# RWKV recurrence of a hybrid block: two pairs of matmul pieces issued as one piece each, with a new table of scheduling offsets

## The chip, the cores and the metric

The kernel runs on one core of a Trainium2 chip. The core has a matmul engine (PE, with its weight loads shown as PEld), a vector engine (DVE), a scalar engine (ACT), a general engine (POOL) and a queue that issues transfers (SP). Each works through its own list of instructions in the order in which the program gives them, and waits on semaphores for the others. The metric is the device time of one execution in microseconds (us); lower is better.

## The reference, cut to what matters

The program computes two layers of a block with three branches (windowed attention, an RWKV-7 recurrence, retention), a gated mix of them, and a feed-forward part, for 256 tokens and a model width of 1024, in float32. The change touches the recurrence, which has 8 heads of 64 columns:

```python
def step(S, inp):
    r_t, w_t, k_t, v_t, a_t, b_t = inp
    Sa = jnp.einsum('bhvk,bhk->bhv', S, a_t)
    S = S * w_t[:, :, None, :] + Sa[..., None] * b_t[:, :, None, :] + v_t[..., None] * k_t[:, :, None, :]
    return S, jnp.einsum('bhvk,bhk->bhv', S, r_t)
_, y = lax.scan(step, S0, xs)
mu = jnp.mean(y, axis=-1, keepdims=True)
var = jnp.mean(jnp.square(y - mu), axis=-1, keepdims=True)
y = ((y - mu) * lax.rsqrt(var + RWKV_LN_EPS)).reshape(B, T, RWKV_WIDTH)
y = y * lnx_g + lnx_b
y = (y + bonus) * g
```

The result of this branch is multiplied by `w_rwkv_o` and goes into the mix.

## The kernel before, in words

**Big matmuls.** Nearly all the work is matrix products with large weights. Each weight block of 512 KB is loaded into `raw`, ACT rounds it to the fast float format (`wh`), DVE takes the rest (`wl = raw - wh`), and PE multiplies three times (`wh` with the high part of the activations, `wl` with the high part, `wh` with the low part) to keep float32 accuracy. These are the matmuls whose weights or moving operand are `wh` or `wl`; there are 3984 of them, and they are called the big matmuls here. Their outputs are named by the product: `gt` the gates, `po` the three output projections, `px` the output of the mix, `pfg`, `pfu`, `pd` the feed-forward part, `pf`, `aq`, `rq`, `rk`, `rv`, `rg` the input projections. (`pd` is also the name of a small tile of the recurrence.)

**Small pieces.** Everything else on PE (transposes, attention scores, the recurrence) is put between big matmuls.

**The order.** The program is first recorded, operation by operation (`Program.add`), and then put in order by a list scheduler that knows the engines, the buffers and rough costs (`forward`). For each engine it takes the ready operation with the highest key. For most small operations the key is the length of the work that still hangs on it plus an offset by the name of the output, from the table `PRI` (line 31). The order is fixed when the program is built: on the chip an engine takes its instructions in this order, whatever happens. `rec.together()` records the matmuls in its block as one operation, which the scheduler can't cut.

**The recurrence** is done in four chunks of 64 tokens (lines 1097 to 1148), each a chain: `pr` (the state with the keys, 8 matmuls of 64 columns) is copied to `RS` by ACT; `pu` multiplies `RS` by `M`, the inverse of the chunk's triangular matrix; ACT and DVE copy `pu` into `sv`, which then holds u beside the state; `pd` multiplies `sv` for the next state, and DVE scales that into the next chunk's `sv` (`SV`). The outputs are `py` (the state with r, 8 matmuls, copied into `ysb` by ACT) and `py2` (`sv` with `GR`, 8 matmuls, added to `ysb` by DVE). In the trace `py2` appears as `py` with `GR` as an operand.

**Behind the recurrence**, for each half t of the tokens, DVE takes the mean from `ysb` (`gmu`), ACT squares (`gsq`), DVE sums (`gvr`), POOL takes the power -1/2 (`ggr`), DVE multiplies by `ab` (made from `pgt`, the gate, and `lnx`), by `ggr`, and adds the other half of `ab`. PE transposes the result (`pto`, 4 transposes), ACT rounds it (`obh`) and DVE takes the rest (`obl`). Then come the big matmuls `po` with `obh` and `obl`. Half 0 of a weight block is multiplied by 6 big matmuls, then half 1 by 6.

All instructions that the scheduler emits carry line 454, the line of `emit`; so the views are read by tile names.

## Time and profile before

| what | before |
|---|---|
| median of 3 runs (lowest to highest) | 955.47 us (954.79 to 955.87) |
| the profiled execution: its own time, its span | 956.34 us, 954.5 us |
| mean granted PE clock | 1.000 |
| PE busy | 946.6 us, 99% of the span |
| DVE, ACT, POOL busy | 673.1, 532.5, 39.7 us |

Rows of the timeline give start, duration, engine, line, operation, output and inputs, shapes and a count of merged instructions; a bracket gives the idle time of that engine ahead of the row and what ended it. PE starts a matmul while the one before is still in the array, so the pace is read from starts, not from durations. A float32 matmul shows as two records: the 8 matmuls of `pr` are `x16`. A plain transpose is one record.

### The profile page before, as it was taken

The numbers are of one execution on the slowest core, as the hardware profiler recorded it, in microseconds if no ns is written. First come the engines' busy times: TensorE is split into PE (matmuls) and PEld (weight loads), VectorE is DVE, ScalarE is ACT, GpSimd is POOL, SyncE is SP. The second block draws the span as 40 slices with busy tenths as digits, with TensorE's granted clock in tenths as the row PEclk, the third lists the DMA queues.
The fourth block names the chain that finished last, engine by engine and source line by source line (L and its number), as shares of the span: only waits on it lengthen the run. The fifth ranks groups of instructions, "written<-read, shape, count | busy, mean of one in ns | idle before, by whom it ended". The sixth has DMA issues, their size and how long they took to land.

```text
span 954.5 us, 15127 instructions
## 1 busy us (share of the span) xinstructions
PE 946.6 (99%) x5906; PEld 791.4 (83%) x5906; DVE 673.1 (71%) x1030; ACT 532.5 (56%) x851; POOL 39.7 (4%) x37
## 2 busy tenths in 40 slices
PE   8999999999999999999999999999999999999998
PEld 6998787877888888898889988888778878888886
DVE  5889889878777555555468799988698665555443
ACT  6875876364547444444468757644645564444332
POOL 1110000000100000000010100000010000000000
PEclk9999999999999999999999999999999999999999
DMA  8656444543655666655553663545535556666562
GB/s 253 188 146 188 118 145 135 154 155 100 192 183 158 198 190 184 186 180 187 184 179 122 177 177 89 177 133 155 155 97 192 176 177 189 186 183 191 178 208 101
DMA packets 93425, 159.04 MB, mean 167 GB/s; under 512 B 5830, under 2 KB 26666, under 8 KB 93354
## 3 DMA queue, kind: packets, MB, share of 16 engines
q1 hardware_dynamic: 93354, 158.08, 54.7%
q8 instruction: 46, 0.75, 0.3%
q14 instruction: 25, 0.20, 0.1%
HBM read 157.01 MB, written 1.05 MB: 166 GB/s over the span
## 4 chain that ended last, share of the span: by engine, by line
PE 94%; DMA 2%; ACT 1%; DVE 1%; issue 1%; SPq 0%; ACTq 0%
PE gt L454 14%; PE pd L454 13%; PE pfu L454 11%; PE pfg L454 11%; PE po L454 8%; PE pf L454 8%; PE px L454 5%; PE rg L454 2%; PE rv L454 2%; PE rk L454 2%; PE rq L454 2%; PE akv L454 1%; DMA raw<-in_w_in_dram 1%; PE aq L454 1%; PE pas L454 1%; PE ptf L454 1%
## 5 line engine op out<-in xcount | busy, mean ns | idle before, releaser
L454 DVE TENSOR_TENSOR wl<-raw,wh 128x1024 fp32r<-128x1024 f32 (+1 forms) x293 | 356.8, 1219 | 208.7 <-ACT wh L454 207.7
L454 ACT CAST wh<-raw 128x1024 fp32r<-128x1024 f32 (+1 forms) x293 | 306.3, 1047 | 311.6 <-PE pd L454 66.3
L454 PE MATMUL gt<-wh,hth 128*128 128x512 f32 x192 | 77.2, 402 | 0.0
L454 PE MATMUL gt<-wh,htl 128*128 128x512 f32 x192 | 76.5, 398 | 0.0
L454 PE MATMUL gt<-wl,hth 128*128 128x512 f32 x192 | 76.3, 398 | 0.0
L454 PE MATMUL pfg<-wl,hth 128*128 128x512 f32 (+1 forms) x192 | 72.6, 378 | 0.0
L454 PE MATMUL pfg<-wh,hth 128*128 128x512 f32 (+1 forms) x192 | 72.2, 376 | 0.0
L454 PE MATMUL pfg<-wh,htl 128*128 128x512 f32 (+1 forms) x192 | 71.7, 373 | 0.0
L454 PE MATMUL pfu<-wl,hth 128*128 128x512 f32 (+1 forms) x192 | 71.4, 372 | 0.0
L454 PE MATMUL pfu<-wh,htl 128*128 128x512 f32 (+1 forms) x192 | 71.3, 371 | 0.0
L454 PE MATMUL pfu<-wh,hth 128*128 128x512 f32 (+1 forms) x192 | 71.3, 371 | 0.0
L454 PE MATMUL pd<-wh,atl 128*128 128x512 f32 x176 | 69.3, 394 | 0.0
L454 PE MATMUL pd<-wh,ath 128*128 128x512 f32 x176 | 69.3, 394 | 0.0
L454 PE MATMUL pd<-wl,ath 128*128 128x512 f32 x176 | 69.1, 393 | 0.0
L454 PE MATMUL pf<-htl,wh 128*128 128x256 f32 x224 | 64.0, 286 | 0.0
L454 PE MATMUL pf<-hth,wl 128*128 128x256 f32 x224 | 63.9, 285 | 0.0
L454 PE MATMUL pf<-hth,wh 128*128 128x256 f32 x224 | 63.8, 285 | 0.0
L454 PEld LDWEIGHTS pf<-htl,wh 128*128 128x128 f32 x224 | 42.8, 191 | 0.4 <-issue 0.3
L454 PEld LDWEIGHTS pf<-hth,wl 128*128 128x128 f32 x224 | 42.8, 191 | 0.4 <-issue 0.3
L454 PEld LDWEIGHTS pf<-hth,wh 128*128 128x128 f32 x224 | 42.8, 191 | 0.1
L454 PEld LDWEIGHTS gt<-wl,hth 128*128 128x128 f32 x192 | 36.1, 188 | 7.6 <-issue 0.6
L454 PEld LDWEIGHTS gt<-wh,hth 128*128 128x128 f32 x192 | 36.1, 188 | 7.6 <-issue 0.2
(326 smaller groups left out, 1927.4 us busy)
## 6 DMA issues: line engine op xcount, KB each, us to landing
raw<-in_w_in_dram SPq DMA_DIRECT2D x119, 512.0 KB, 3.9
raw<-in_w_ffn_gate_dram SPq DMA_DIRECT2D x44, 512.0 KB, 4.1
raw<-in_w_ffn_up_dram SPq DMA_DIRECT2D x44, 512.0 KB, 3.7
raw<-in_w_ffn_down_dram SPq DMA_DIRECT2D x44, 512.0 KB, 3.6
raw<-in_w_out_dram SPq DMA_DIRECT2D x16, 512.0 KB, 3.6
raw<-in_w_attn_o_dram SPq DMA_DIRECT2D x8, 512.0 KB, 3.6
raw<-in_w_ret_o_dram SPq DMA_DIRECT2D x8, 512.0 KB, 3.7
raw<-in_w_rwkv_o_dram SPq DMA_DIRECT2D x8, 512.0 KB, 3.6
```

The lines of the kernel that those rows point to most:

```text
L454: fn(*args, **kw)
```

## The change

Three things change.

1. In each chunk, `py` is recorded in the same piece as `pr`, and `py2` in the same piece as `pd` (in the last chunk, where there is no `pd`, `py2` is alone). The number of matmuls stays.
2. The copies of `pu` into `sv` are recorded ahead of the copies of `py` into `ysb`.
3. `PRI` holds other offsets for other names, so the order changes in the whole program, not only in the recurrence.

```diff
 PRI = {
-    "PC": -83000, "Tn": -20000, "Y": 60000, "Zs": 16000, "amx": -8000, "cum": 49000, "gsq": 23000, "k2":
...
+    "M": -2000, "Sb": -20000, "Tt": 65000, "ab": -16000, "adn": -3000, "ass": -51000, "bv": -3000,
...
                 with rec.together():
-                    for p in range(4):
-                        for par in range(2):
-                            mm(pr[HR[par], p, :], X[p][:, par, c, 0:64], sv[:, p, par, :])
+                    for p, par in heads:
+                        mm(pr[HR[par], p, :], X[p][:, par, c, 0:64], sv[:, p, par, :])
+                    for p, par in heads:
+                        mm(py[HR[par], p, :], X[p][:, par, c, 64:128], sv[:, p, par, :])
                 RS = ST([128, 4, 64], "RS")
                 S.copy(RS, pr)
-                py = PS([128, 4, 64], "py")
-                with rec.together():
...
                 pu = PS([128, 4, 64], "pu")
...
+                S.copy(sv[HR[0], :, 0, :], pu[HR[0]])
+                V.tensor_copy(sv[HR[1], :, 1, :], pu[HR[1]])
                 yv = ysb[t].rearrange("p (a b) v -> p a b v", b=2)
                 for par in range(2):
                     S.copy(yv[rr, :, par, :], py[HR[par]])
-                S.copy(sv[HR[0], :, 0, :], pu[HR[0]])
-                V.tensor_copy(sv[HR[1], :, 1, :], pu[HR[1]])
...
+                with rec.together():
+                    for p, par in heads if c < 3 else ():
+                        mm(pd[HR[par], p, :], BKT[p // 2][:, p % 2, c, 64 * par:64 * par + 64], sv[:, p, par, :])
+                    for p, par in heads:
+                        mm(py2[HR[par], p, :], GR[HR[par], p, c, :], sv[HR[par], p, par, :])
...
-                py2 = PS([128, 4, 64], "py2")
-                with rec.together():
...
```

What the scheduler makes of it is seen where instructions stand. First PE in one chunk of the recurrence of layer 2, before; `gt` and `po` are big matmuls, the other rows the pieces of the chunk, and the last row is `py2`:

```order
L454 MATMUL pr<-SV,X 64x64 x8
L454 MATMUL py<-SV,X 64x64 x8
L454 MATMUL gt<-wl,hth 128x512
L454 MATMUL gt<-wh,htl 128x512
L454 MATMUL pu<-RS,M 64x64 x8
L454 MATMUL gt<-wh,hth 128x512
L454 MATMUL gt<-wl,hth 128x512
L454 MATMUL gt<-wh,htl 128x512
L454 MATMUL gt<-wh,hth 128x512
L454 MATMUL gt<-wl,hth 128x512
L454 MATMUL pd<-SV,BKT 64x64 x8
L454 MATMUL py_1200<-SV,GR 64x64 x8
```

The same chunk now, up to `pu`:

```order
L453 MATMUL pr<-SV,X 64x64 x8
L453 MATMUL py<-SV,X 64x64 x8
L453 MATMUL po<-wh,ocl 128x512
L453 MATMUL po<-wh,och 128x512
L453 MATMUL po<-wl,och 128x512
L453 MATMUL po<-wh,ocl 128x512
L453 MATMUL pu<-RS,M 64x64 x8
```

`py` stood right behind `pr`, and `py2` right behind `pd`, before the change too, in all 8 chunks and in all 6 that have a `pd`. What moved is the distance: four big matmuls between `py` and `pu` where there were two, and the last `py2` of layer 2 stands behind 2948 big matmuls of the program where it stood behind 2904.

Second, PE at the end of the branch in layer 2, before; `pto_1231` are the transposes of half 1, `po_1461` the product for half 0, `po_1462` that for half 1:

```order
L454 MATMUL pto_1231<-cst_105,ysb_1185 128x128 x4
L454 MATMUL po_1461<-wh_1464,obh_1220 128x512
L454 MATMUL po_1461<-wl_1465,obh_1220 128x512
L454 MATMUL po_1461<-wh_1464,obl_1221 128x512
L454 MATMUL po_1461<-wh_1464,obh_1220 128x512
L454 MATMUL po_1461<-wl_1465,obh_1220 128x512
L454 MATMUL po_1461<-wh_1464,obl_1221 128x512
L454 MATMUL po_1462<-wh_1464,obh_1220 128x512
```

The same place now:

```order
L453 MATMUL po_1461<-wh_1464,obh_1220 128x512
L453 MATMUL po_1461<-wl_1465,obh_1220 128x512
L453 MATMUL po_1461<-wh_1464,obl_1221 128x512
L453 MATMUL pto_1231<-cst_105,ysb_1185 128x128 x4
L453 MATMUL po_1461<-wh_1464,obh_1220 128x512
L453 MATMUL po_1461<-wl_1465,obh_1220 128x512
L453 MATMUL po_1461<-wh_1464,obl_1221 128x512
L453 MATMUL po_1462<-wh_1464,obh_1220 128x512
```

Between `pto_1231` and the first matmul that needs its result stood six big matmuls; now there are three. From the last `py2` to `pto_1231` stood 96 big matmuls; now there are 55.

Third, DVE ahead of `pto_1231` in layer 2, before; `ysb_1185` is half 1, `ysb_1184` half 0, `wl` belongs to the big matmuls:

```order
L454 TENSOR_REDUCE gvr_1229<-gsq_1228 128x8
L454 TENSOR_TENSOR ysb_1185<-ysb_1185,ab_1219 128x512
L454 TENSOR_TENSOR wl_1455<-raw_1453,wh_1454 128x1024
L454 TENSOR_SCALAR gvr_1229<-gvr_1229 128x8
L454 TENSOR_TENSOR ysb_1184<-ysb_1184,ab_1216 128x512
L454 TENSOR_TENSOR mix_1335<-mix_1335,tg_1419 128x512
L454 TENSOR_TENSOR mix_1336<-mix_1336,tg_1420 128x512
L454 TENSOR_TENSOR wl_1458<-raw_1456,wh_1457 128x1024
L454 TENSOR_TENSOR obl_1221<-pto_1226,obh_1220 128x4x128
L454 TENSOR_TENSOR ysb_1185<-ysb_1185,ggr_1230 128x512
L454 TENSOR_TENSOR wl_1465<-raw_1463,wh_1464 128x1024
L454 TENSOR_TENSOR ysb_1185<-ysb_1185,ab_1219 128x512
```

And now:

```order
L453 TENSOR_TENSOR ab_1216<-bv_1215,pgt_1214 128x512
L453 TENSOR_REDUCE gvr_1229<-gsq_1228 128x8
L453 TENSOR_TENSOR wl_1458<-raw_1456,wh_1457 128x1024
L453 TENSOR_TENSOR ysb_1185<-ysb_1185,ab_1219 128x512
L453 TENSOR_SCALAR gvr_1229<-gvr_1229 128x8
L453 TENSOR_TENSOR ysb_1184<-ysb_1184,ab_1216 128x512
L453 TENSOR_TENSOR wl_1465<-raw_1463,wh_1464 128x1024
L453 TENSOR_TENSOR ysb_1185<-ysb_1185,ggr_1230 128x512
L453 TENSOR_TENSOR ab_1219<-bv_1218,pgt_1217 128x512
L453 TENSOR_TENSOR obl_1221<-pto_1226,obh_1220 128x4x128
L453 TENSOR_TENSOR wl_1468<-raw_1466,wh_1467 128x1024
L453 TENSOR_TENSOR ysb_1185<-ysb_1185,ab_1219 128x512
```

The two `mix` additions stand elsewhere, the second halves of `ab` stand in this stretch now, and three `wl` stand between the sum `gvr_1229` and the last addition, as before.

## The prediction

> **What bounds the kernel now.** I read the page first: busy times, the chain that ended last, then PE's waits.

> ```profile
> PE 946.6 (99%) x5906; PEld 791.4 (83%) x5906; DVE 673.1 (71%) x1030; ACT 532.5 (56%) x851; POOL 39.7 (4%) x37
> PE 94%; DMA 2%; ACT 1%; DVE 1%; issue 1%; SPq 0%; ACTq 0%
> ```

> PE is busy nearly the whole span and makes up 94% of the chain. Busy PE records overlap, so this alone does not say that nothing waits. The view of who waited for whom, for PE alone, does:

> ```profile
> PE akv L454 <- DVE wl L454: 0.7, 1, 0.7
> PE ptf L454 <- DVE sl L454: 0.4, 1, 0.4
> PE pss L454 <- ACT kq L454: 0.3, 1, 0.3
> ```

> Beside 0.7 us near the start (`akv`), PE waits for 0.4 and 0.3 us in a span of 954.5; the view's other two rows lie in the first microseconds. So the time is the sum of PE's work. A change of order can do two things: alter the number of places where PE turns from big matmuls to small pieces, or bring a wait where there is none. A recurrence chain that gets shorter gains nothing by itself, since PE never waits for it.

> **The pieces in the recurrence.** The timeline of PE in a chunk gives the price of a visit to narrow matmuls (those that use a part of the 128x128 array):

> ```profile
> 210.06 0.39 PE L454 MATMUL gt<-wl,hth 128*128 128x512 f32 x1
> 210.37 0.69 PE L454 MATMUL pd<-SV,BKT 128*64 128x64 f32 x16
> 210.99 0.68 PE L454 MATMUL py<-SV,GR 64*64 64x64 f32 x16
> 211.60 0.50 PE L454 MATMUL gt<-wh,htl 128*128 128x512 f32 x1
> ...
> 212.40 0.40 PE L454 MATMUL gt<-wh,htl 128*128 128x512 f32 x1
> 212.72 0.69 PE L454 MATMUL pr<-SV,X 128*64 128x64 f32 x16
> 213.24 0.64 PE L454 MATMUL py<-SV,X 128*64 128x64 f32 x16
> 213.81 0.50 PE L454 MATMUL gt<-wh,hth 128*128 128x512 f32 x1
> 214.14 0.40 PE L454 MATMUL gt<-wl,hth 128*128 128x512 f32 x1
> 214.47 0.68 PE L454 MATMUL pu<-RS,M 64*64 64x64 f32 x16
> 215.08 0.50 PE L454 MATMUL gt<-wh,htl 128*128 128x512 f32 x1
> ```

> A big matmul alone takes 0.23 from start to start. From 212.40 to 213.81 are 1.41, so `pr` and `py` together cost 1.18. `pu` alone: 215.08 - 214.14 - 0.23 = 0.71. Two single visits would be 1.42, the double one is 1.18, so a visit costs 0.24 beyond its matmuls. The big matmul behind it then takes 0.33 (213.81 to 214.14) instead of 0.23, another 0.10 to 0.11. A visit is 0.35 us.

> Would the merged pieces save visits? They would if `py` stood apart. The order shows `py` right behind `pr` in all 8 chunks and `py2` right behind `pd` in all 6, before as after. The pieces cost zero: the scheduler did by itself what the change prescribes. The copies of `pu` that are recorded earlier cost nothing either: the order between engines' own lists is set by keys, and ACT is 56% busy.

> `pd` with `py2` costs 211.60 - 210.06 - 0.23 = 1.31, 0.13 more than `pr` with `py`: the first pair turns from 128\*64 to 64\*64 inside, the second stays in 128\*64. [...]

> **What the new order does to the number of visits.** Counted in the order of PE, before and now, as uninterrupted runs of narrow matmuls: `pw`/`pa` 2 and 3, `pg`/`pgk` 6 and 7, `pm` 6 and 8, `poa` 7 and 5, all others 32 and 32. That makes 53 and 55: two more, 2 x 0.35 = +0.7. Stretches of any small work between big matmuls fall from 173 to 164. For transposes that is nearly neutral, so I take nothing and keep ±0.5 in the range; the bound is nine visits' 0.11, about 1.0 less.

> **Waits that could come.** They are looked for where a result now has fewer big matmuls to hide behind. The clearest place is the end of the branch in layer 2: 55 big matmuls between the last `py2` and `pto_1231` (before 96), and three between `pto_1231` and its first reader (before six). What PE and DVE need there, from the same place before:

> ```profile
> 701.93 0.68 PE L454 MATMUL py<-SV,GR 64*64 64x64 f32 x16
> 702.55 1.98 PE L454 MATMUL pgt<-g,sg 128*128 128x512 f32 x4
> 703.97 0.79 PE L454 MATMUL gt<-wh,hth 128*128 128x512 f32 x1
> 704.60 0.40 PE L454 MATMUL gt<-wl,hth 128*128 128x512 f32 x1
> ...
> 726.44 0.40 PE L454 MATMUL gt<-wh,htl 128*128 128x512 f32 x1
> 726.68 0.60 PE L454 MATMUL pto<-cst,ysb 128*128 128x128 f32 x4
> 727.03 0.48 PE L454 MATMUL po<-wh,obh 128*128 128x512 f32 x1
> 727.35 0.39 PE L454 MATMUL po<-wl,obh 128*128 128x512 f32 x1
> ...
> 728.96 0.39 PE L454 MATMUL po<-wh,obl 128*128 128x512 f32 x1
> ```

> ```profile
> 706.78 0.42 DVE L454 TENSOR_TENSOR ysb<-ysb,py 64x256 f32<-64x256 f32 x1
> 707.13 1.22 DVE L454 TENSOR_TENSOR wl<-raw,wh 128x1024 fp32r<-128x1024 f32 x1
> 708.26 0.68 DVE L454 TENSOR_REDUCE gvr<-gsq 128x8 f32<-128x512 f32 x1
> ...
> 719.08 0.17 DVE L454 TENSOR_SCALAR gvr<-gvr 128x8 f32<-128x8 f32 x1
> 719.15 0.69 DVE L454 TENSOR_TENSOR ysb<-ysb,ab 128x512 f32<-128x512 f32 x1
> 719.75 1.29 DVE L454 TENSOR_TENSOR mix<-mix,tg 128x512 f32<-128x512 f32 x2
> ...
> 728.07 0.69 DVE L454 TENSOR_TENSOR obl<-pto,obh 128x512 fp32r<-128x512 f32 x1 [1.41 <-ACT obh L454]
> ```

> ```profile
> 709.89 2.47 POOL L454 TENSOR_TENSOR ggr<-gvr,cst 128x8 f32<-128x8 f32 x1 [45.30 <-DVE gvr L454]
> 719.32 2.01 POOL L454 TENSOR_TENSOR ggr<-gvr,cst 128x8 f32<-128x8 f32 x1 [6.96 <-DVE gvr L454]
> 727.46 0.58 ACT L454 CAST obh<-pto 128x512 fp32r<-128x512 f32 x1
> ```

> PE's way from the start of the last `py2` to the start of `pto_1231`: 2.04 to the first `gt` (703.97 - 701.93), 0.40 that this `gt` takes beyond 0.23, 55 x 0.227 = 12.5, and 0.45 for the first `pto` (726.44 to 727.35 is 0.91 for two big matmuls and it). Together 15.4.

> DVE's way is a row of steps, from start to start: a 128x512 operation 0.60 (719.15 to 719.75), a `wl` 1.13, a 64x256 one 0.35, a small one 0.07. The first `pgt` result comes about 1.7 after `py2` starts (between 1.6, half of the 1.98 behind 702.55, and 2.3, when DVE used it before). In the new order follow, up to the scaled `gvr_1229`, nine 128x512 steps (5.40), one 64x256 (0.35), two `wl` (2.26), and two small ones, the last to its end (0.24): 8.25. POOL's power takes 2.01 to 2.47, with about 0.1 to start. Then three 128x512 steps, a `wl` and the last addition to its end: 1.80 + 1.13 + 0.69 = 3.62, and 0.1 to PE. Sum 15.8 to 16.3. `pto_1231` is 0.4 to 0.9 late, 0.3 to 1.5 with the bounds of the start; I take 0.8, near the upper end, because DVE must also have cleared what stands ahead.

> Then the way through `obh` and `obl`. Before, `obl` ended at 728.76 and its first reader started at 728.96: 0.20 to spare. Three big matmuls fewer are 0.69, so it is 0.49 short, or 0.35 if ACT starts `obh` as soon as it can (before, it began 0.18 behind the end of `pto`, 727.28). I take 0.45. **This end costs 1.25 us** (bounds 0 and 2.1; a gain is excluded, since PE had no wait there to lose).

> In the front of layer 2 three `pss` pieces now stand one big matmul apart (before 10 and more), right behind the ACT operations that feed them; the one `pss` wait of 0.3 was of this kind. A `wl` wait is possible there too, of the kind that cost 0.7 at `akv`. I take 0.7 for both, less the 0.3 that goes: +0.4 (from -0.3, if only the old wait goes, to 1.0). In layer 1 the same end has 74 big matmuls between the last `py2` and its second `pto`, and eight, not three, before that one's first reader; that is 19 x 0.227 = 4.3 us more than in layer 2 up to `pto` alone, so zero there.

> **Sum.** 0.7 + 1.25 + 0.4 = +2.35, so the span goes from 954.5 to 956.9 and the profiled execution from 956.34 to 958.7. Its own time is 0.87 above the median of the three timed runs; from the median 955.47 the forecast is **957.8 us**. A measurement of this kernel tells about 0.2%, 1.9 us, from no change; the forecast is a little beyond that.

> **Rivals.**
> - *DVE is early enough and the end of layer 2 shows no wait.* For it: the scheduler counts its costs itself and could have seen the wait. Against it: 15.8 to 16.3 against 15.4 from measured steps. Then +0.7 + 0.4 = 956.6, no change that can be told. 0.30.
> - *DVE enters the end later.* If the `wl` ahead of it is not done when `pgt` comes, its 1.13 adds to the lateness: 957.8 + 1.1 = 958.9 and with a second one 960.0. For it: my 1.7 for the first `pgt` may be as much as 2.3 by the bound above. 0.11.
> - *DVE steps do not overlap.* If each step took its full 0.69 instead of 0.60, some 15 steps would add 15 x 0.09 = 1.35: 959.2. The trace's 719.15 to 719.75 speaks against it. [...] 0.03.
> - *Faster: fewer stretches.* Nine stretches fewer save 0.11 each behind them, 1.0; the `pss` and `ptf` waits go, 0.7; the start of the kernel, with the 0.7 at `akv`, gets smoother. With no wait at the end and the visits unpriced that is 955.47 - 2.4 = 953.1. It decides if more than 1.9 of this comes without the two visits. Against it: the visits are counted, and the start's order is hardly touched. 0.05. That the merging itself saves 14 x 0.35 = 4.9 (950.6) is excluded by the order: the 14 pairs stood together; 0.01.

> **How the numbers follow.** The forecast has 0.50, with its own range 956.7 to 959.2; about a tenth of it (0.05) lies within 0.2%. Faster: 0.05 + 0.01 = 0.06. Same: 0.30 + 0.05 = 0.35. Slower: 0.45 + 0.11 + 0.03 = 0.59. The range reaches from 955.4, below the first rival with its unpriced stretches, to 960.2, the second `wl`; what lies outside is the faster rival and a bit at each end.

> **What would show it.** In the new profile: PE waits for `ysb` (at `pto`), `obh` and `obl` near 730 us, together about 1.2 us, and none in layer 1; a `pss` wait near 530; 55 visits at 0.35; `pr` and `py` still at 1.18. If those waits are under 0.3 us in sum, the step with 15.4 against 16.3 is wrong; if the time falls below 953.5, PE's sum is not what sets it, or visits are cheaper than read; if it is over 960.4, a wait came at a place that I did not look at.

## The result, and the profile after

| | before | after |
|---|---|---|
| median (lowest to highest) | 955.65 us (954.79 to 955.87, 4 runs) | 960.8 us (960.32 to 962.1, 4 runs) |
| profiled execution: own time, span | 956.34, 954.5 us | 962.1, 960.0 us |
| mean granted PE clock | 1.000 | 0.998 |

The changed kernel is slower: ratio 1.0057, 95% interval 1.0045 to 1.0069, so 5.2 us (4.3 to 6.6). The forecast was 957.8, with a range up to 960.2: the sign was right, the size less than half.

The page's busy row and its chain, after:

```profile
PE 950.1 (99%) x5906; PEld 793.6 (83%) x5906; DVE 671.4 (70%) x1030; ACT 533.8 (56%) x851; POOL 39.8 (4%) x37
PE 95%; DMA 2%; DVE 1%; ACT 1%; issue 0%; SPq 0%; ACTq 0%
```

PE is still what the kernel is made of. The view of who waited for whom, PE alone (us in total, times, longest):

```profile
PE pss L453 <- ACT kq L453: 1.2, 1, 1.2
PE aq L453 <- ACT hth L453: 1.1, 1, 1.1
PE pto L453 <- DVE ysb L453: 0.7, 1, 0.7
```

`pss` waits 1.2 us instead of 0.3, `pto` waits 0.7 instead of 0; `ptf`'s 0.4 is gone, and `akv`'s 0.7 has shrunk to 0.14, under what the view lists. `aq` waits in the first 10 us, where the profiled runs differ from each other without any edit (below).

**Where the time arises.** The 3984 big matmuls stand in the same order in both kernels, so the start of the same one can be compared. At the places of the table PE has the same small pieces behind it in both. Worked out from the timelines, after minus before:

| big matmul no. | where | before, us | after, us | after - before |
|---|---|---|---|---|
| 0 | first `aq` | 7.42 | 7.50 | 0.07 |
| 400 | projections, layer 1 | 72.37 | 73.16 | 0.79 |
| 1000 | behind the recurrence, layer 1 | 254.49 | 254.70 | 0.21 |
| 1710 | end of `pfu`, layer 1 | 416.37 | 416.59 | 0.22 |
| 2100 | front of layer 2 | 500.60 | 501.31 | 0.71 |
| 2400 | projections, layer 2 | 544.52 | 548.49 | 3.98 |
| 2800 | retention done, layer 2 | 661.03 | 664.93 | 3.89 |
| 2998 | ahead of `pto` | 726.22 | 730.57 | 4.36 |
| 3100 | `px`, layer 2 | 751.98 | 757.83 | 5.85 |
| 3250 | `pfg`, layer 2 | 789.53 | 794.63 | 5.11 |
| 3983 | last `pd` | 950.44 | 955.97 | 5.53 |

Two places carry most of the loss: the front of layer 2 (+3.27 from no. 2100 to 2400) and the end of its recurrence (+1.49 from 2998 to 3100).

**The pieces.** The timeline of PE in a chunk of layer 1, after:

```profile
214.43 0.39 PE L453 MATMUL gt<-wl,hth 128*128 128x512 f32 x1
214.75 0.69 PE L453 MATMUL pr<-SV,X 128*64 128x64 f32 x16
215.26 0.64 PE L453 MATMUL py<-SV,X 128*64 128x64 f32 x16
215.83 0.50 PE L453 MATMUL gt<-wh,htl 128*128 128x512 f32 x1
...
216.95 0.68 PE L453 MATMUL pu<-RS,M 64*64 64x64 f32 x16
```

From 214.43 to 215.83 less 0.23 is 1.17: the pair costs on PE what it cost before, 1.18. But `pu` starts 2.20 behind `pr`; before it was 1.75 (212.72 to 214.47).

**The end of layer 2**, timeline of PE, after:

```profile
716.31 0.68 PE L453 MATMUL py<-SV,GR 64*64 64x64 f32 x16
...
731.50 0.39 PE L453 MATMUL po<-wh,obl 128*128 128x512 f32 x1
732.61 0.63 PE L453 MATMUL pto<-cst,ysb 128*128 128x128 f32 x4 [0.72 <-DVE ysb L453]
...
733.54 0.40 PE L453 MATMUL po<-wh,obl 128*128 128x512 f32 x1
733.91 0.50 PE L453 MATMUL po<-wh,obh 128*128 128x512 f32 x1
734.25 0.40 PE L453 MATMUL po<-wl,obh 128*128 128x512 f32 x1
734.77 0.50 PE L453 MATMUL po<-wh,obl 128*128 128x512 f32 x1
```

PE would have been ready for `pto` at 731.73 (0.23 behind 731.50), 15.4 behind `py2`; it starts at 732.61, 16.3 behind. The next `obh` and `obl` show as starts that are 0.37 and 0.52 apart where 0.23 is the pace. DVE's timeline at the same place, where the first row waits for POOL's power and a `wl` stands ahead of the last addition:

```profile
728.84 0.69 DVE L453 TENSOR_TENSOR ysb<-ysb,ggr 128x512 f32<-128x512 f32 x1 [0.39 <-POOL ggr L453]
...
730.64 1.22 DVE L453 TENSOR_TENSOR wl<-raw,wh 128x1024 fp32r<-128x1024 f32 x1
731.78 0.68 DVE L453 TENSOR_TENSOR ysb<-ysb,ab 128x512 f32<-128x512 f32 x1
```

**The front of layer 2**, timeline of PE, after:

```profile
528.92 0.28 PE L453 MATMUL pf<-hth,wl 128*128 128x256 f32 x1
530.36 0.61 PE L453 MATMUL pss<-cst,kq 128*128 128x2 f32 x4 [1.16 <-ACT kq L453]
...
532.79 0.85 PE L453 MATMUL pss<-cst,kq 128*128 128x2 f32 x4
...
534.07 0.41 PE L453 MATMUL pf<-hth,wh 128*128 128x256 f32 x1
534.28 0.41 PE L453 MATMUL pf<-htl,wh 128*128 128x256 f32 x1
```

The wait is 1.16 us. What the forecast did not have at all is behind it: the same `pf` matmuls, 0.12 apart elsewhere, are 0.21 apart here. The windows say why (length, busy times of PE, PEld, DVE, ACT, POOL, the granted PE clock, then the DMA engines' share and GB/s):

```profile
529.00:530.40 1.40, 0.24 (x3) 0.05 (x1) 0.51 (x3) 1.40 (x4) 0.00 (x0) 1.00 0.57 162
530.40:532.40 2.00, 2.00 (x18) 2.00 (x18) 0.76 (x4) 2.00 (x5) 0.00 (x0) 1.00 0.66 220
532.40:535.80 3.40, 3.40 (x19) 3.40 (x18) 0.73 (x2) 3.40 (x11) 1.88 (x1) 0.50 0.00 0
```

Two microseconds after the wait PE gets half its clock, for 3.4 us. Why `kq` is late is seen on ACT:

```profile
526.09 1.05 ACT L453 CAST wh<-raw 128x1024 fp32r<-128x1024 f32 x1 [1.95 <-DMA raw<-in_w_in_dram]
527.15 1.28 ACT L453 ACT_TABLE_LOAD   x1
528.45 1.06 ACT L453 ACTIVATE EN<-cum 128x1024 f32<-128x1024 f32 x1
529.41 0.49 ACT L453 ACTIVATE zr<-hs,omu 128x256 f32<-128x256 f32 x1
529.81 1.29 ACT L453 ACTIVATE kq<-zk,vec 128x256 f32<-128x256 f32 x3
```

`kq` takes its buffer behind `EN` (one pool, handed out in recorded order), and `EN` needs the four scans `cum` and these the eight `pw`/`pa` pairs. Before, PE did the pairs in one visit; after, in two, 4.4 us apart. That is only a part of it. `tw`, which the scans read, is scaled 6.6 us later (517.34, before 510.74). Then DVE puts other work between the scans:

```profile
518.41 1.27 DVE L453 TENSOR_TENSOR_SCAN cum<-cst,tw 128x256 f32<-128x256 f32 x2
...
521.66 0.68 DVE L453 TENSOR_TENSOR_SCAN cum<-cst,tw 128x256 f32<-128x256 f32 x1
...
524.63 0.68 DVE L453 TENSOR_TENSOR_SCAN cum<-cst,tw 128x256 f32<-128x256 f32 x1
```

They end at 525.31, 8.0 us behind the start of the scaling; before it was 4.7 (510.74 to 515.47). The old table gives `cum` an offset of +49000, the new one none. Last, the `wh` at 526.09, which `EN` does not need, stands ahead of it on ACT and waits 1.95 us; so `EN` starts 3.1 behind the end of the last scan (before 2.2). No run tries these three apart. ACT reaches `EN` only at 528.45 (before at 517.67), three of the four `kq` come together, and three of the four pieces of `pss` stand one big matmul apart.

### The profile page after: what moved, and what is told of

Its sections match the earlier page's. It is cut to its first block, busy times and chain, and to the rows that moved or that the text cites. A ratio compares the mean times of both kernels' runs of the same rounds, so it can differ in the third digit from the quotient of the medians.

```text
span 960.0 us, 15131 instructions
## 1 busy us (share of the span) xinstructions
PE 950.1 (99%) x5906; PEld 793.6 (83%) x5906; DVE 671.4 (70%) x1030; ACT 533.8 (56%) x851; POOL 39.8 (4%) x37
## 4 chain that ended last, share of the span: by engine, by line
PE 95%; DMA 2%; DVE 1%; ACT 1%; issue 0%; SPq 0%; ACTq 0%
PE gt L453 14%; PE pd L453 13%; PE pfg L453 13%; PE pfu L453 13%; PE po L453 8%; PE pf L453 7%; PE px L453 5%; PE rg L453 2%; PE rv L453 2%; PE rq L453 2%; PE rk L453 2%; DMA raw<-in_w_in_dram 2%; PE akv L453 1%; PE aq L453 1%; PE pas L453 1%; PE ptf L453 1%
## 5 line engine op out<-in xcount | busy, mean ns | idle before, releaser
L453 PEld LDWEIGHTS gt<-wh,htl 128*128 128x128 f32 x192 | 36.1, 188 | 7.6 <-issue 0.5
```

The source lines that it names most:

```text
L453: fn(*args, **kw)
```

## The experiments

Theory A: the new offsets make the loss, by the waits that they bring; merging is neutral. Theory B: the longer pieces themselves make the branch end later, whatever the table. Two questions came up on the way: what the half clock costs (A: 1.6 us; C: nothing), and whether places can be mended one by one (A) or a gain in one is given back in the next (D).

The first eight columns of numbers are the lag behind the kernel before at the same big matmul, in the profiled runs (us). At no. 1000 e2_offsets_only and e5_prpy_only have one `pto` piece more behind them than the others, about 0.35 us (what it takes from its start to the next in the kernel before, 726.68 to 727.03):

| kernel | no. 1000 | 1130 | 2100 | 2400 | 2800 | 2998 | 3100 | 3983 | median, us | ratio to before |
|---|---|---|---|---|---|---|---|---|---|---|
| changed | 0.21 | 0.24 | 0.71 | 3.98 | 3.89 | 4.36 | 5.85 | 5.53 | 960.8 | 1.0057 (1.0045 to 1.0069) |
| e1_merge_only | -0.29 | 1.24 | 1.27 | 1.26 | 1.26 | 1.43 | 4.43 | 4.09 | 961.58 | 1.0065 (1.0048 to 1.0082) |
| e2_offsets_only | 1.45 | 1.01 | 1.44 | 5.93 | 5.84 | 6.52 | 8.13 | 7.55 | 962.17 | 1.0072 (1.0057 to 1.0087) |
| e3_front_old | -0.39 | -0.34 | 0.14 | 0.16 | 1.35 | 2.66 | 4.26 | 3.66 | 960.46 | 1.0049 (1.0034 to 1.0064) |
| e5_prpy_only | 0.37 | -0.06 | -0.09 | -0.09 | -0.09 | -0.05 | 1.57 | 0.77 | 957.23 | 1.0015 (1.0005 to 1.0024) |
| e6_pdpy_only | 0.96 | 2.52 | 2.31 | 2.36 | 2.36 | 2.41 | 4.08 | 4.29 | 959.62 | 1.0040 (1.0025 to 1.0054) |
| e8_front_tail_visits | 0.04 | 0.07 | 0.77 | 0.77 | 2.00 | 2.12 | 2.13 | 1.80 | 957.84 | 1.0022 (1.0013 to 1.0032) |

### Merging without the new table, and the table without merging

e1_merge_only is the changed kernel with the old `PRI`; e2_offsets_only the kernel before with the new one.

> The merged pieces and the earlier copies of the changed kernel, with the table of offsets of the kernel before. Theory A (the loss comes from the new offsets alone; merging is neutral because the pairs stood together before): no change against before, 955.7 +- 0.7 us, PE waits behind the recurrence of layer 2 below 0.3 us, clock 1.000. Theory B (a longer piece that the scheduler can't cut changes what stands between the chunks, so the branch ends later under any table): 958 to 960 us, with PE waits for ysb, obh and obl behind the recurrence, over 1.5 us together.

> The code of the kernel before with the new table of offsets: pr, py, pd and py2 are four pieces again. Theory A (the offsets carry the loss): 960.8 +- 0.7 us, with the wait of pss for kq of about 1.2 us in the front of layer 2 and the clock at 0.998. Theory B (the longer piece carries the end of the branch): the front's part stays, 3 us (0.9 of the wait, 1.6 of the half clock behind it, 0.5 of the split pw/pa and a wl wait), the waits at the end of the branch go: 958.6 us.

Measured: 961.58 and 962.17 us. Theory A falls for the first, B for the second, and in size both fall short: B had at most 960 for the first, A at most 961.5 for the second. Each half of the change alone costs 6.0 or 6.6 us, both together 5.2; the two costs do not add up. PE's waits at the ends of the branch in e1_merge_only:

```profile
PE pto L455 <- DVE ysb L455: 2.2, 1, 2.2
PE po L455 <- DVE obl L455: 0.6, 1, 0.6
PE po L455 <- ACT obh L455: 0.4, 1, 0.4
```

In layer 1 the waits for `obh` and `obl` (1.0 us) cost 1.5 (no. 1000 to 1130), in layer 2 the wait for `ysb` 2.2 and with what follows 3.0 (2998 to 3100). So merging is not neutral, and the new table is in part a repair of it: with it layer 1 ends without a wait, and `pto` waits 0.7 instead of 2.2. But the table brings the front of layer 2 with it, also where nothing is merged (e2_offsets_only: +4.5 from no. 2100 to 2400, with a wait of 0.9 for `kq` and half the clock for 6.8 us).

### Which merged piece

The old table, and one of the two merges. e5_prpy_only:

```diff
+                py = PS([128, 4, 64], "py")
                 with rec.together():
-                    for p in range(4):
-                        for par in range(2):
-                            mm(pr[HR[par], p, :], X[p][:, par, c, 0:64], sv[:, p, par, :])
+                    for p, par in heads:
+                        mm(pr[HR[par], p, :], X[p][:, par, c, 0:64], sv[:, p, par, :])
+                    for p, par in heads:
+                        mm(py[HR[par], p, :], X[p][:, par, c, 64:128], sv[:, p, par, :])
                 RS = ST([128, 4, 64], "RS")
                 S.copy(RS, pr)
-
-                py = PS([128, 4, 64], "py")
-                with rec.together():
-                    for p in range(4):
-                        for par in range(2):
-                            mm(py[HR[par], p, :], X[p][:, par, c, 64:128], sv[:, p, par, :])
```

e6_pdpy_only does the same for `pd` and `py2` alone.

> The kernel before with its own table, and one edit of three: py is recorded in one piece with pr; pd and py2 stay two pieces. Merging everything under the old table cost 5.9 us (961.58 against 955.62), so it is not neutral; this asks which piece does it. Theory B (the scheduler believes that RS can be copied only when the whole piece is done, so it puts pu about two big matmuls later in every chunk, 0.45 us, and the branch ends later under an unchanged pto): waits at the end of layer 2 of about 1.5 us, none in layer 1, 957.5 us. Rival: the pair costs nothing by itself and all of it comes from pd with py2: 955.6 us.

> The kernel before with its own table, and one edit of three: py2 is recorded in one piece with pd; pr and py stay two pieces. Theory B (DVE's scaling of pd into the next state is believed to come only after py2, and is put behind one more wl, so a chunk gets longer): waits for obh and obl at the end of both layers, about 1.5 us each, 958.5 us. Rival: it costs nothing by itself, 955.6 us.

Measured: 957.23 (+1.7) and 959.62 (+4.1); the sum, 5.9, is what merging both cost (961.58 - 955.62 = 6.0). Theory B holds for both, with waits where it put them: e5_prpy_only only at the end of layer 2 (+1.62 from no. 2998 to 3100), e6_pdpy_only at both ends (+1.56 from 1000 to 1130, +1.67 from 2998 to 3100); e6_pdpy_only is 1.1 above what it named. How, the timelines show. The kernel before, from `RS` to `pu`:

```profile
692.72 0.37 ACT L454 COPY RS<-pr 128x256 f32<-128x256 f32 x1 [0.16 <-PE pr L454]
693.66 0.68 PE L454 MATMUL pu<-RS,M 64*64 64x64 f32 x16
```

and e5_prpy_only:

```profile
693.55 0.38 ACT L455 COPY RS<-pr 128x256 f32<-128x256 f32 x1 [2.50 <-PE pr L455]
694.97 0.68 PE L455 MATMUL pu<-RS,M 64*64 64x64 f32 x16
```

In both chunks `RS` is copied as soon as `pr` is there, 0.8 behind its start. But the scheduler counts a piece as one operation: for it `RS` can begin only when `py` is done too, so it puts two more big matmuls ahead of `pu`: 1.42 from `RS` to `pu` instead of 0.94. With `pd` and `py2` it is DVE's order. Before, the new state comes right behind `Sb`:

```profile
689.83 0.42 DVE L454 TENSOR_TENSOR Sb<-pd,Sn 128x256 f32<-128x256 f32 x1 [1.52 <-PE pd L454]
690.29 0.87 DVE L454 TENSOR_TENSOR SV<-Sb,PC 64x256 f32<-64x256 f32 x2
```

and in e6_pdpy_only an addition of `py2`, which the scheduler takes to be ready at the same time, goes first:

```profile
692.44 0.42 DVE L455 TENSOR_TENSOR Sb<-pd,Sn 128x256 f32<-128x256 f32 x1 [0.91 <-PE pd L455]
693.05 0.42 DVE L455 TENSOR_TENSOR ysb<-ysb,py 64x256 f32<-64x256 f32 x1 [0.19 <-PE py L455]
693.50 0.87 DVE L455 TENSOR_TENSOR SV<-Sb,PC 64x256 f32<-64x256 f32 x2
```

`SV` starts 1.06 behind `Sb` instead of 0.46. Chunks that last longer leave fewer big matmuls behind the last one: between the last `py2` and the second `pto` of layer 2 stand 80 in e5_prpy_only and 83 in e6_pdpy_only, before 96.

### The front of layer 2

e3_front_old: the old offsets for the operations of that front alone (`i` is an operation's number in recorded order, `FRONT` the old table).

```diff
-            if o["name"] in PRI:
-                return (2, bl[i] + PRI[o["name"]])
+            tab = FRONT if 3500 <= i < 4330 else PRI
+            if o["name"] in tab:
+                return (2, bl[i] + tab[o["name"]])
```

> The changed kernel, but for the operations in the front of layer 2 (its norm, attention, input projections and decay, up to where the recurrence's blocks are transposed) the offsets of before hold; all else has the new ones. Theory A (one wait of 1.16 us in that front, and the half clock for 3.2 us behind it, are the biggest part of the loss): 960.8 - 0.9 - 1.6 - 0.3 (split pw/pa) - 0.2 (wl) = 957.8 us, pss wait at most 0.3, clock 1.000, tail waits unchanged at about 1.3. Theory C (the low clock in the record costs nothing by itself, or comes back at another place): only the wait and the split go, 959.4 to 959.6, or the clock stays at 0.998.

Measured: 960.46 us. As expected, the front is then as it was before (+0.02 from no. 2100 to 2400, clock 1.000), 3.25 less than in the changed kernel. But the median is only 0.3 lower, 0.7 against e11_after_again below, and the span of the profiled run 1.8. So neither theory's time came (957.8, or 959.4 to 959.6). The end costs 1.6 (in the changed kernel 1.5), which was expected. What was not: 1.2 between no. 2400 and 2800, where the same small pieces now go into other places (`ptp` waits 0.3 for `X`), while the changed kernel gains 0.1 there; and 1.3 from there to no. 2998 (0.5 in the changed kernel), of it 0.7 in which PE stands still inside a merged piece with no wait that the profile shows. The first is the gain given back further on, theory D below; the second came up in other kernels too, and not in every run.

### The half clock

e4_fill gives PE something to do in the wait:

```diff
-            ph = PS([128, 2, 4, 2], name)
+            full = PS([128, 512], name)
+            ph = full[:, 0:16].rearrange("p (t a b) -> p t a b", t=2, a=4)
...
+                    if name == "pss" and l == 1 and p == 0 and t == 0:
+                        fill = dict(lhsT=ident, rhs=ident, start=True, stop=True)
+                        rec.ops[-1]["calls"] = [(nc.tensor.matmul, (full[:, 0:128],), fill)] * FILL + rec.ops[-1]["calls"]
```

> The changed kernel with five more matmuls of 128 x 128 (float32, about 0.2 us each) ahead of the first pss of layer 2, in the place where PE waits for kq; what they write is overwritten by pss. The order of all else is the same, and kq comes as late as before. Theory A (PE standing still is what halves the clock, and the half clock costs 1.6 us): the wait falls to about 0.1 us but the time at which pss starts is the same, the clock stays at 1.000, 960.8 - 1.6 = 959.2 us (bounds 958.9 and 959.6). Theory C (the dip is not from the idle time, or costs nothing): 960.8 us or up to 1 us more.

Measured: 959.94 us (959.58 to 961.5), 0.9 below the changed kernel, between what A (958.9 to 959.6) and C (960.8 or more) had named. The two were timed on different occasions, so they were run once more side by side, with six extra matmuls:

> The changed kernel once more, without an edit, on the same chip and in the same rounds as the next one, since e4_fill and the changed kernel were timed on different occasions and single runs spread over 1.5 us. Expected of it by all theories: 960.8 +- 0.5 us, a mean clock of 0.998 in most runs (one period of 3.4 us at half in about 960).

> As e4_fill, with six extra matmuls instead of five (1.3 us of work where PE waits for kq, so that a wait of up to 1.3 us is covered). Theory A (the half clock behind the wait costs 1.6 us in nearly every run): 1.4 to 1.6 us less than e11_after_again, clock 0.999 to 1.000 in nearly all runs. Theory C (the dip is rare, or a matter of the profiled run): at most 0.5 us less.

Measured: 961.14 and 959.92 us, 1.2 less, five runs each; their ranges overlap (959.74 to 963.47 and 959.13 to 960.83). The windows of e12_fill_again at the same place:

```profile
529.00:530.40 1.40, 1.40 (x15) 1.40 (x14) 0.82 (x4) 1.40 (x5) 0.00 (x0) 1.00 0.71 195
532.40:535.80 3.40, 3.40 (x32) 3.40 (x30) 1.19 (x2) 3.40 (x12) 2.40 (x1) 1.00 0.04 13
```

PE is busy where it stood still, and the clock stays at 1.00: 32 matmuls fit where the changed kernel had 19. `kq` comes 0.5 earlier in this profile, but the extra matmuls hold the first `pss` that reads it until 530.42, as late as in e11_after_again (530.39). At big matmul no. 2400 the lag is 2.44 against 4.05 there, so in these two traces the dip is worth 1.6 us, as theory A had it; the medians, 1.2 apart, lie between A's 1.4 and C's 0.5.

In the 9 runs of the changed kernel the mean clock was 0.996 to 0.998 in seven, 0.999 in one and 1.000 in one (that one took 959.74 us); of the 5 of e12_fill_again four had 1.000 and one 0.999, and the kernel before shows 0.999 or 1.000. So the dip is not rare, and that part of C is out. One more kernel bears on its price: of the four runs of e1_merge_only two had 1.000 (960.76 and 960.88 us) and two 0.998 (962.27 and 962.52), 1.6 us apart, though no trace of the slower two was kept. In e2_offsets_only the same step, from 1.000 (961.76) to 0.998 (962.14 and 962.21), is only 0.4 us, so single runs do not give the price.

How long must PE stand still? e9_gaps puts waits among big matmuls of the kernel before (`GAPS`: unit of a weight block, number of copies).

```diff
+                if self.ops[i]["bulk"] and GAPS.get(self.ops[i]["unit"], 0):
+                    held = self.ops[i]["calls"][0][2]["lhsT"]
+                    for _ in range(GAPS.pop(self.ops[i]["unit"])):
+                        self.nc.scalar.copy(held, held.bitcast(F32))
```

> The kernel before, with waits put into the dense feed-forward part: at ten places 22 to 24 us apart, ACT writes a block of 128 x 128 of the activations back onto itself 4 to 12 times, so that the next matmul, which reads it, has to wait. Five such waits in layer 1 (4, 5, 6, 7, 8 copies) and five in layer 2 (4, 5, 7, 9, 12). By the aks casts of the trace, 0.27 us each, the waits should be some 0.4 to 3.3 us. The question is how long PE must stand still among big matmuls to be granted half the clock. Theory E (about 1.2 us are enough anywhere, as at pss): half the clock for 3.4 us behind each wait over 1.2 us, six or seven dips, each 1.7 us. Theory F (what counts is how little PE did in one period of 3.4 us; at pss the wait came together with three pss pieces of little work): waits up to about 1.5 us among big matmuls leave the clock at 1.000, and only the longest, over 2 us, cost it. [...]

Measured (a single run, 965.44 us): six of the ten became waits of PE that show, 5.9 us together. The two longest:

```profile
854.89 0.39 PE L459 MATMUL pfu<-wh,htl 128*128 128x512 f32 x1
856.54 0.50 PE L459 MATMUL pfu<-wh,hth 128*128 128x512 f32 x1 [1.26 <-ACT hth L457]
856.87 0.39 PE L459 MATMUL pfu<-wl,hth 128*128 128x512 f32 x1
857.11 0.40 PE L459 MATMUL pfu<-wh,htl 128*128 128x512 f32 x1
```

```profile
881.78 0.50 PE L459 MATMUL pfu<-wh,hth 128*128 128x512 f32 x1 [2.25 <-ACT hth L457]
882.13 0.44 PE L459 MATMUL pfu<-wl,hth 128*128 128x512 f32 x1
882.37 0.63 PE L459 MATMUL pfu<-wh,htl 128*128 128x512 f32 x1
882.79 0.63 PE L459 MATMUL pfu<-wh,hth 128*128 128x512 f32 x1
```

Behind the wait of 1.26 the pace is 0.24 from the second matmul on and the clock 1.00 (856.60 to 860.00); behind the one of 2.25 it is 0.42, with half the clock:

```profile
882.30:885.80 3.50, 3.50 (x10) 2.71 (x10) 1.98 (x2) 0.38 (x1) 0.00 (x0) 0.51 0.17 54
```

The other four waits are 2.4 us together, and the run's mean clock, 0.998, is what the one dip of 3.5 us makes. That speaks for theory F: 1.26 us among big matmuls brought no half clock, while 1.16 us at `pss`, followed by pieces of little work, cost 1.6 more. But the length of the wait and the work around it do not settle it alone. In the trace of e1_merge_only PE stands still for 2.18 us ahead of `pto`, among big matmuls too, and the clock is 1.00 in every window of 1 us from 10 to 950 us. What decides, and where the border lies, is left open.

### The end of layer 2

e7_wl_behind changes the order of DVE there.

```diff
         order = self.order = self.schedule()
+        dve = [i for i in order if self.ops[i]["eng"] == "DVE"]
+        for name in ("ysb", "obl"):
+            op = max(i for i in dve if self.ops[i]["name"] == name)
+            wl = max((i for i in dve[:dve.index(op)] if self.ops[i]["name"] == "wl"), key=dve.index)
+            order.remove(wl)
+            order.insert(order.index(op) + 1, wl)
```

> The changed kernel, with two wl of the end of layer 2 put behind the operations in front of which they stood on DVE: one behind the last addition to ysb, one behind the last obl. All else stands in the same order. Theory A (DVE's queue, a wl of 1.2 us ahead of the last ysb, makes pto wait): PE's wait for ysb goes from 0.7 to 0, the waits for obh and obl stay at 0.3 to 0.8 together because only three big matmuls lie between pto and its reader; the stretch around pto gets 0.7 us shorter. Rival (POOL's power, or the wl that now come later, set the end): the waits stay at 1.0 us or PE waits for wl.

Measured (a single run): `pto` no longer waits, one wait of 0.4 for `obh` is left, and the stretch from big matmul 2998 to 3100 adds 0.83 to the lag (6.73 to 7.56) instead of 1.49: 0.7 less, theory A. So it was DVE's queue, a `wl` ahead of the last addition, that held `pto`. The run as a whole, 963.8 us, says nothing of this edit: its wait for `kq` was 1.3 us, with half the clock for 6.8 us behind it.

### Mending the places together

e8_front_tail_visits:

```diff
+            tab = PRI if i < 3500 else FRONT if i < 4330 else REST
```

with `PRI` the new table and `ptv` +40000, `FRONT` the old one, `REST` the new one with `ptv` +40000, `ptb` +30000, `t1` -70000.

> The changed kernel with three tables: the new one in layer 1 with ptv +40000 (one visit of pm less per layer), the old one in the front of layer 2, and behind that the new one with ptb +30000, ptv +40000 and t1 -70000, chosen so that more big matmuls lie between the last py2 and pto. Theory A (the loss is a sum of places that can be mended one by one: front 3.0 by the profile, end 1.9, two visits 0.7): 956.0 +- 0.7 us, no wait of PE over 0.5 us behind the first 30 us. Theory D (what PE saves in the front it waits for further on, since the chain of the recurrence does not start earlier, as the kernel with the old front alone gained only 0.3): 958.5 us or more, with waits of PE in the recurrence or behind it.

Measured: 957.84 us, between the two theories: 2.35 above the kernel before in the same rounds (955.49), where the changed kernel had 5.15. The front (+0.0) and the end (+0.0) are mended. What is left in the profiled run is 1.2 between no. 2400 and 2800, with the small pieces in the middle of layer 2 at other places, and 0.65 and 0.42 in the two down projections, less 0.75 between no. 3100 and 3250.

e10_each_its_layer takes each layer from where it came out best: merged pieces under the new table (with `ptv` +40000) in layer 1, the four separate pieces under the old table in layer 2.

> A version put together from the stages that came out best: in layer 1 the merged pieces with the new table and ptv +40000 (its stretch from the projections to the recurrence was 0.6 to 0.8 us shorter than before), in layer 2 the four separate pieces with the old table (no wait at the front but the 0.3, none at the end). Theory A (stages add up): 955.5 - 0.8 = 954.7 us, or up to 955.6 if the down projections are 0.5 to 0.9 us slower as in all kernels with the new table. Theory D (an edit in one layer comes back as a wait in the other): over 956.5 us.

Measured: 956.93 us against 956.26 for the kernel before in the same rounds, ratio 1.0005 (0.9996 to 1.0014): no difference that can be told. Theory A's 954.7 to 955.6 was missed, and the waits of theory D did not come either: behind the first 30 us PE waits only the 0.3 at `pss`. In the profiled run layer 1 does gain 0.8 from no. 400 to 1000, but 1.0 is lost ahead of it and 1.25 in the down projections. No version tried beats the kernel before.

## Why the prediction was too small

- **PE's work sets the time**: held; 99% busy, 95% of the chain.
- **Merging costs zero, the earlier copies too** (step "the pieces"): wrong. On PE the pair does cost what it cost, and nothing was gained since the pairs stood together. But from "PE's row is the same" I went on to "the order is the same". Both merges alter when the scheduler believes the consumers can start, and under the old table that is worth 1.7 and 4.1 us. The copies alone were not tried. In the sum the effect was contained, because the 55 big matmuls were counted in the order that had it; the cause was not seen.
- **Two visits more, +0.7, stretches neutral**: mis-sized. From no. 400 to 1000 the changed kernel gained 0.58, from 2400 to 2800 0.09, from 2800 to 2998 it lost 0.47, and the second `pw`/`pa` visit is part of the front. That fits nine stretches fewer that took back about what the two visits cost, but no run shows it; I had put them at zero with a bound of -1.0.
- **The end of layer 2, +1.25 (0 to 2.1)**: right in mechanism and near in size, 1.49. PE's way (15.4) was met; `pto` was to be 0.8 late and waits 0.72, and with `obh` and `obl`, put at 0.45, the rest is 0.6. That DVE's way came to 16.3, the upper end, is partly luck: the steps up to the scaled `gvr` took 8.64 instead of 8.25, and POOL's power the lower of the two times, 2.01.
- **The front of layer 2, +0.4 (-0.3 to 1.0)**: the step that failed. The place and the wait were named, "three `pss` pieces one big matmul apart". But I priced it by the one wait of the kind that the old trace showed, 0.3, and by a `wl` wait. It is +3.27 in the profile: 0.9 more of waiting, 1.6 of half clock, and some 0.8 for the second `pw`/`pa` visit (which the forecast counted with the visits), the `wl` wait of 0.15 and the pieces standing close. What was missing is the chain ahead of `kq`: `pw`/`pa` in two visits, the scans apart on DVE and a waiting `wh` on ACT, so `EN` late by 10.8 us, and then the clock, which nothing in the old trace showed below 1.00. The time came out above 960.4, which was to mean a place not looked at; it was looked at, and priced too low.
- **`ptf`**: its wait is gone, and the stretch from no. 3100 to 3250 is 0.74 shorter; I had this only in a rival.
- **Down projections**: +0.9 us that no step had, from no. 1710 to 2100 (0.49) and from 3700 to the end (0.43). The same matmuls stand in the same order, each nearly 2 ns slower (0.92 us over some 530). It is there, between 0.6 and 1.3 in sum, in all kernels with the new table in layer 1, and not (at most 0.1 in sum) in those with the old one. The cause stays open.
- **The start**: +0.7 at no. 400 in the profiled run. This part differs between profiled runs (from -0.4 to +1.0 in the kernels here, 0.2 to 0.9 where layer 1 has the same order), and it may be part of why the profiled run lies 1.3 above the median.
- **The rivals**: that the end shows no wait (0.30) did not happen. Nor was DVE late at the entry (0.11): it stood idle 0.28 us for the first `pgt` at 718.08, 1.8 behind `py2`, where the forecast had 1.7. The `wl` that e7_wl_behind took away is the one that the forecast's sum had ahead of the last `ysb`.

The sum by place, 0.79 start, -0.58 layer 1, 0.49 and 0.43 down projections, 3.27 front, 0.38 between the front and no. 2998, 1.49 end, -0.74 `ptf`, is 5.53, the difference of the two spans.

## What to carry to other kernels

When pieces are merged for a list scheduler, look not at whether they were adjacent but at who reads the first half: the planner will hold that reader until the second half is done, and may put other work ahead of it on its own engine. A wait on the matmul engine is priced with what follows it: behind the 1.16 us at `pss` the clock was 0.50 for 3.4 us, 1.6 us more, while behind 2.18 us in e1_merge_only it stayed at 1.00, so the windows behind a wait have to be read too. And where the order was tuned as a whole, what is mended at one place can be lost at the next, as in e3_front_old, so an edit is judged by the whole time, not by its place.
